# Final stage of a streaming encoder step: row scaling in two operations, its sums and low halves on POOL, and another order of loads and of the last block

## The chip, the cores and the metric

The kernel runs on one core of one Trainium2 chip. The core has five engines with a queue of their own each: PE (TensorE, matrix products), DVE (VectorE), ACT (ScalarE), POOL (GpSimd) and SP (SyncE, which here issues nearly all DMAs). Each engine works off its instructions in the order in which the program holds them, and waits for other engines on semaphores. Data lies in SBUF (128 partitions), products collect in PSUM banks of 512 fp32 columns. The metric is the device time of one execution in microseconds; less is better. One execution was also recorded by the hardware profiler, and all rows below come from that record.

## The reference

One step of a trunk layer over 2048 prompt rows and 32 sample rows of width 1024. Attention and a gated delta rule read the same normalised input; each of the two gives a branch output. What matters here is the end of the layer:

```
h   = layer_norm(x, ln0_g, ln0_b)                 # the residual stream
mix = sigmoid(gate_a) * ya + sigmoid(gate_b) * yb # two branches, each a product with its own weights
y   = layer_norm(ALPHA * h + mix @ w_out, ln_g, ln_b)
```

`ya` and `yb` are the branch operands (width 512 each) times `w_branch_a` and `w_branch_b` (512 x 1024); `w_out` is 1024 x 1024. The prompt and the sample rows pass through the same formulas with caches and states of their own.

## The kernel before, in words

Most of the span computes the input projection, the attention and the delta rule. The change lies in the last 270 us, from 1710 us on, which the program calls by these parts:

**Branch units** (`early`, `branch`). The branch operand g is loaded from memory (`glo`), cast to a high half `ghi` on ACT, and the rest `glo` is formed by a subtraction on POOL or VectorE (`split_g`). Each g buffer serves a unit: for every one of eight column tiles of 128, up to two times 256 columns, 12 products per 256 columns (whi and wlo with ghi, whi with glo). The result is multiplied on VectorE by the gate (`sg`, later `sl`), which was loaded from `sig`, and written back there. The units of the second branch still run between the first blocks of the stage below. Their PSUM bank carries the tag `b`.

**Final stage** (`merge`). The 2048 rows go in eight blocks of 256. For each of eight tiles k of 128 activation columns, `load` brings both gated branches (`sf`, 2 x 256 columns), and `fold` adds them (the sum), casts the sum to the high half `mh` on ACT and subtracts to get the low half `ml`. Sum and low half were made on VectorE for even tiles and on POOL (low half only) for odd ones. TensorE then makes, for two row tiles t and two column halves c, three products of 512 columns per k: mh with the high and the low part of `w_out`, ml with the high part. That is 96 products of 512 columns per block. The weights are `wohi`, `wolo` for k = 0 to 3 and `woh`, `wol` for k = 4 to 7. The last block also holds the 32 sample rows, with their high and low halves in one operand `ms`, 32 products.

**Banks.** PSUM tiles have the tags `a` (three banks), `c` (one), `pj` (two) and `b` (two). While branch units remain, blocks use a, a and a, c; afterwards blocks alternate between pj, b and a, c. A block's two row tiles run side by side through k, but in the last block the tiles follow each other: sample rows first, in bank b, then the first 128 rows in pj, then the others in a.

**Rows** (`x_ahead`, `x_load`, `finish`). An `xt` buffer, five in all, holds 128 rows of x. `x_load` loads them, subtracts the mean and multiplies by the reciprocal deviation (`mv`, known from the start of the kernel) on VectorE, and then scales by ln0's vectors `l0g` and `l0b`, which are already multiplied by ALPHA, in eight operations of 256 columns each: on VectorE for the first two tiles and on POOL for all others. `finish` adds the products out of PSUM to it (the eviction, which frees the bank), takes the statistics (`fst`), makes the deviation (`m`, a square root by power on POOL), scales by the final `lng` and `lnb` in two VectorE operations of 1024 columns, and stores the rows. Then the xt buffer is free for the next load.

**Weights and vectors** (`last_weights`). The second half of `w_out`, k = 4 to 7, is staged in three of the xt buffers (named `wr` then) and in the buffer of `lnb`, cast on ACT and split on POOL or VectorE. After the eight loads come l0g and l0b, and after those the first x tiles; lng and lnb come last.

**What sets the order.** The instruction stream is written at build time by a planner in Python (`Flow`). Each of the functions above is a stream that gives up control after each step; the planner always continues the stream with the smallest clock, puts its instruction at the end of the engine's queue, and moves the clocks on by a table of costs. Gates (`x_slots`, `m_slots`, `bank`) and marks hold streams back. So one change of a step can move many others in all queues. At run time nothing is reordered. All compute instructions are issued from one line, L267, and all DMAs from L290, so rows of the profile are told apart by the names of their tiles.

Of the kernel before, what the change touches and what calls it, by code (L numbers as in the profile page):

```python
# [16 lines left out]
ALU = mybir.AluOpType  # L17
# [4 lines left out]
P = 128  # L22
D = 1024
# [252 lines left out]
def trunk(ctx: ExitStack, tc: tile.TileContext, x_p, x_s, cache_k, cache_v, st_conv, st_gdn,  # L276
# [4 lines left out]
    flow = Flow()  # L281
# [1828 lines left out]
    def last_weights():  # L2110
# [20 lines left out]
        def scale(r, t, last):  # L2131
            yield t
            S.activation(out=r, in_=r, func=AF.Copy, scale=ALPHA)
            if last:
                rows_ready.done()

        stage = x_t + [rowv["lnb"][:]]
        for i in range(2 * KO, 2 * KD):
            yield from load(i // 2, i % 2, stage[i // 2 - KO][:, i % 2 * 512:(i % 2 + 1) * 512])
        for name, src in (("l0g", ln0_g), ("l0b", ln0_b)):  # L2140
            yield from row(name, src)
        flow.start(x_ahead())
        for k in range(KO, KD - 1):
# [82 lines left out]
    def early():  # L2226
        while True:
# [12 lines left out]
            for f in range(KD):  # L2240
# [5 lines left out]
                while fp_open.at is None and flow.busy["PE"] > flow.cur.clock + 0.2:  # L2246
                    yield flow.busy["PE"]
                yield bank["b"]
                ps = pt("b")
                for i, ((_, g, _), m) in enumerate(zip(what, sizes)):  # L2250
                    yield from branch(br, f, m, ps[:, i * FB:], g)

                def evac(f=f, sg=sg, slots=slots, ps=ps, t=t, c0=c0, n=n, what=what, br=br):
                    yield t + SLACK
                    V.scalar_tensor_tensor(out=sg[:, 0:n], in0=sg[:, 0:n], scalar=1.0, in1=ps[:, 0:n],
                                           op0=ALU.add, op1=ALU.mult)
                    bank["b"].give()
                    yield
                    at = dma(sig_dram[br][f][:, c0:c0 + n], sg[:, 0:n])
                    for b, _, _ in what:  # L2260
                        early_done[br, b, f].done()
                    yield at
                    slots.give()
# [21 lines left out]
    def merge():  # L2285
# [20 lines left out]
        def fold(B, f, sg, t):  # L2306
            n, x = B.n, sg[:, 0]
            yield t + SLACK / 2
            V.tensor_tensor(out=x[:, 0:n], in0=x[:, 0:n], in1=sg[:, 1, 0:n], op=ALU.add)
            yield  # L2310
            yield m_slots[f]
            eng = G if f % 2 else V
            S.copy(out=mh[f][:], in_=x[:, 0:FB])
# [56 lines left out]
        B = blocks[-1]  # L2370
        for t, name in ((2, "ba"[turn_]), (0, ("pj", "a")[turn_]), (1, ("a", "pj")[turn_])):
            yield from rows(B, (t,))
            for c in range(2):
                yield bank[name]
# [10 lines left out]
    def x_ahead():  # L2385
        n = SEQ // P
        for gt in [*range(n - 2), n, n - 2, n - 1]:
            yield x_slots
# [4 lines left out]
    def x_load(w, gt, rows):  # L2393
# [5 lines left out]
        yield rows_ready  # L2399
        V.tensor_scalar(out=xt[:rows], in0=xt[:rows], scalar1=mv[:rows, gt, 0:1],  # L2400
                        scalar2=mv[:rows, gt, 1:2], op0=ALU.subtract, op1=ALU.mult)
        yield
        eng = V if gt < 2 else G

        for name, op in (("l0g", ALU.mult), ("l0b", ALU.add)):
            for q in range(4):
                cs = slice(q * 256, (q + 1) * 256)
                eng.tensor_tensor(out=xt[:rows, cs], in0=xt[:rows, cs], in1=rowv[name][:rows, cs], op=op)
            yield
        w.ready.done()  # L2410

    def finish(w, gt, rows, c, ps, end, name):
# [11 lines left out]
        if c == 0:  # L2424
# [9 lines left out]
        yield norm_ready  # L2434
        V.scalar_tensor_tensor(out=xt[:rows], in0=xt[:rows], scalar=m2[:rows, 0:1], in1=rowv["lng"][:rows],
                               op0=ALU.subtract, op1=ALU.mult)
        yield
        V.scalar_tensor_tensor(out=xt[:rows], in0=xt[:rows], scalar=m2[:rows, 1:2], in1=rowv["lnb"][:rows],
                               op0=ALU.mult, op1=ALU.add)
        yield  # L2440
        yield dma(y_s if rows < P else y_p[gt * P:(gt + 1) * P, :], xt[:rows])
        x_slots.give()
# [99 lines left out]
```

## Time and profile before

| | us |
|---|---|
| runs shown, lowest, median, highest | 1983.57, 1983.99, 1987.36 |
| profiled execution, its time | 1980.36 |
| its span, first to last instruction | 1978.6 |
| mean granted TensorE clock | 0.988 |
| busy: PE, DVE, ACT, POOL | 1894.8, 1421.8, 993.2, 814.7 |

The profile's first section gives busy time by engine; the second the same in 40 slices of 49.5 us; the third the DMA queues; the fourth the chain of work that ended last, followed back from the last instruction; the fifth groups of instructions with mean duration, the idle time of their engine ahead of them and what ended it (the releaser). A row of the trace gives start, duration, engine, line, operation and tiles (out <- in), partitions x elements and type, and in brackets the idle time before it. A line such as `1838.56:1860.65 22.09, ...` is a stretch of the span: its length, then for each engine the busy time and the number of instructions, then the granted clock, the DMA share and GB/s.

### The profile page before, as it was taken

Reading aid. Unit: us, or ns where it says so; the run is one execution under the profiler, and the core shown is the slowest. Engines: PE = TensorE matmul, PEld = TensorE weight load, DVE = VectorE, ACT = ScalarE, POOL = GpSimd, SP = SyncE. Lnnn points to the kernel's source line nnn. Section 1 sums busy time; section 2 is a strip of 40 time slices with the busy share of each in tenths; the row PEclk is TensorE's granted clock in tenths of the full one; section 3 lists DMA queues with packets and bytes.
Section 4 is the critical chain, followed back from the end, with each engine's and each line's share of the span. In section 5 each row is a group of like instructions: output and inputs, shape, how many; then the busy total and the mean of one; then the engine's idle time right before and its main releaser. Section 6 shows DMA issues by size and latency. Waiting matters only on the chain.

```text
span 1978.6 us, 41065 instructions
## 1 busy us (share of the span) xinstructions
PE 1894.8 (96%) x14513; PEld 1338.2 (68%) x14513; DVE 1421.8 (72%) x4458; ACT 993.2 (50%) x2022; POOL 814.7 (41%) x1139
## 2 busy tenths in 40 slices
PE   8999999999999999999999999999999999989996
PEld 5455666676455556666776777678877668878874
DVE  7779989873378768579989986356466665585886
ACT  6665545444586777664544533445355774310110
POOL 7344334433344444343333432423122331363695
PEclk9999999999999999999999999999999999999998
DMA  4224242333378786223142243578878798975542
GB/s 139 68 83 125 65 108 70 84 92 108 115 159 197 188 179 156 71 79 89 52 118 68 68 112 83 139 212 192 227 173 199 168 215 177 310 272 191 167 152 83
DMA packets 382806, 274.62 MB, mean 139 GB/s; under 512 B 248322, under 2 KB 319342, under 8 KB 382600
## 3 DMA queue, kind: packets, MB, share of 16 engines
q1 hardware_dynamic: 382600, 272.00, 51.3%
q8 instruction: 114, 1.87, 0.4%
q14 instruction: 92, 0.75, 0.1%
HBM read 157.15 MB, written 71.76 MB: 116 GB/s over the span
## 4 chain that ended last, share of the span: by engine, by line
PE 64%; DVE 20%; issue 5%; ACT 4%; DMA 4%; POOL 3%; SPq 1%; POOLq 0%; DVEq 0%; ACTq 0%
PE pj L267 34%; PE b L267 15%; PE a L267 7%; PE c L267 4%; PE x L267 3%; DVE acc L267 3%; DVE sys_t L267 2%; DVE sys_u L267 2%; PE o L267 2%; DVE kd_bd L267 1%; POOL wlo L267 1%; SPq L290 1%; DVE xt L267 1%; DVE q_bd L267 1%; DMA sf<-sig 1%
## 5 line engine op out<-in xcount | busy, mean ns | idle before, releaser
L267 PE MATMUL pj<-hi,whi 128*128 128x512 f16 (+2 forms) x1992 | 642.3, 338 | 11.2 <-DVE zb L267 3.2
L267 PE MATMUL pj<-hi,wlo 128*128 128x512 f16 (+2 forms) x1952 | 633.8, 338 | 0.6 <-POOL wlo L267 0.5
L267 PEld LDWEIGHTS <-whi 128*128 128x128 f16 x3984 | 407.8, 104 | 227.3 <-issue 8.6
L267 POOL TENSOR_TENSOR wlo<-wraw,whi 128x256 f16<-128x256 f32 (+1 forms) x392 | 280.6, 738 | 460.9 <-ACT whi L267 380.5
L267 PE MATMUL pj<-lo,whi 128*128 128x512 f16 (+2 forms) x1992 | 452.5, 338 | 0.0
L267 PEld LDWEIGHTS <-wlo 128*128 128x128 f16 x1952 | 204.3, 105 | 115.2 <-issue 11.9
L267 ACT ACTIVATE sb<-sb,mx,unit 128x640 f32<-128x640 f32 (+4 forms) x128 | 108.6, 849 | 101.4 <-DVE mx L267 96.3
L267 POOL TENSOR_TENSOR pu<-sb,pu 128x640 f16<-128x640 f32 (+2 forms) x64 | 82.3, 1285 | 178.3 <-ACT pu L267 145.4
L267 ACT ACTIVATE wraw<-wraw,w_scale 128x1024 f32<-128x1024 f32 (+1 forms) x98 | 111.4, 1137 | 78.3 <-DVE w_scale L267 75.8
L267 PE MATMUL b<-ghi,whi 128*128 128x256 f32 (+1 forms) x512 | 138.7, 303 | 3.6 <-DVE cr L267 1.1
L267 ACT CAST whi<-wraw 128x512 f16<-128x512 f32 (+2 forms) x212 | 128.2, 611 | 27.5 <-PE pj L267 24.6
L267 PE MATMUL b<-ghi,wlo 128*128 128x256 f32 (+1 forms) x512 | 129.5, 284 | 0.0
L267 DVE TENSOR_TENSOR sys_u<-sys_u,sys_t 128x60 f32<-128x60 f32 (+24 forms) x527 | 124.6, 242 | 5.7
L267 DVE SCALAR_TENSOR_TENSOR acc<-raw,cwT,acc 128x512 f32<-128x512 f32 x144 | 112.7, 782 | 7.9 <-ACT acc L267 6.5
L267 ACT CAST mh<-sf 128x256 fp32r<-128x256 f32 x64 | 25.7, 406 | 178.8 <-PE c L267 74.8
L267 DVE TENSOR_TENSOR sys_t<-sys_u,sys_p 128x60 f32<-128x60 f32 (+21 forms) x459 | 109.8, 242 | 5.5
L267 PEld LDWEIGHTS b<-ghi,whi 128*128 128x128 f32 x512 | 97.3, 190 | 9.7 <-ACT ghi L267 1.5
L267 ACT COPY v_t<-o 128x64 f32<-128x64 f32 x132 | 27.7, 210 | 143.2 <-PE o L267 106.7
L267 PEld LDWEIGHTS b<-ghi,wlo 128*128 128x128 f32 x512 | 97.5, 190 | 1.5
L267 DVE CUSTOM_DVE_ANT_0 sb<-a,bias 128x320 f32<-128x320 f32 (+5 forms) x136 | 66.2, 497 | 45.0 <-PE a L267 42.4
L267 POOL TENSOR_TENSOR w_scale<-w_scale,mhalf 128x1 f32<-128x1 f32 x49 | 32.2, 657 | 157.3 <-DVE w_scale L267 113.8
L267 ACT ACTIVATE sig<-pj,w_half 128x512 f32<-128x512 f32 (+2 forms) x84 | 49.3, 587 | 77.0 <-PE pj L267 71.6
(377 smaller groups left out, 4097.7 us busy)
## 6 DMA issues: line engine op xcount, KB each, us to landing
wraw<-in_w_in SPq DMA_DIRECT2D x192, 256.0 KB
sf<-sig SPq DMA_DIRECT2D x112, 128.0 KB
sig<-sig SPq DMA_DIRECT2D x44, 256.0 KB
sg<-sig SPq DMA_DIRECT2D x37, 256.0 KB
sig<-sg SPq DMA_DIRECT2D x37, 256.0 KB
sys_p<-sol_p SPq DMA_DIRECT2D x68, 128.0 KB
x<-in_x_p SPq DMA_DIRECT2D x16, 512.0 KB
xt<-in_x_p SPq DMA_DIRECT2D x16, 512.0 KB
```

The source lines that it names most:

```text
L267: r = f(*a, **k)
L290: eng.dma_start(dst, src)
```

## The change

Five things are changed, all in the last 270 us:

- `x_load`: the scaling of a tile is two VectorE operations of 1024 columns, (x - mean) * l0g and then times reciprocal deviation plus l0b, for all tiles. POOL has no part in it.
- `fold`: from the second block on, all low halves are made on POOL, and the sums of odd tiles too.
- `last_weights`: l0g and l0b are loaded first and the x tiles are started ahead of the weights of k = 4 to 7. `x_ahead` also puts the sample rows behind one more prompt tile.
- `merge` and `early`: the last block runs the first 128 rows, then the sample rows, then the other 128 rows; branch units use the pj banks once the input projection is done with them (`jobs_done`).
- `finish`: the very last tile's scaling and store go in two halves of 512 columns.

```diff
@@ -2134,12 +2134,12 @@
             if last:
                 rows_ready.done()
 
+        for name, src in (("l0g", ln0_g), ("l0b", ln0_b)):
+            yield from row(name, src)
+        flow.start(x_ahead())
         stage = x_t + [rowv["lnb"][:]]
         for i in range(2 * KO, 2 * KD):
             yield from load(i // 2, i % 2, stage[i // 2 - KO][:, i % 2 * 512:(i % 2 + 1) * 512])
-        for name, src in (("l0g", ln0_g), ("l0b", ln0_b)):
-            yield from row(name, src)
-        flow.start(x_ahead())
         for k in range(KO, KD - 1):
             yield w_ready["o", k, 1]
             x_slots.give()
@@ -2245,16 +2245,17 @@
                         yield m
                 while fp_open.at is None and flow.busy["PE"] > flow.cur.clock + 0.2:
                     yield flow.busy["PE"]
-                yield bank["b"]
-                ps = pt("b")
+                name = "b" if jobs_done.at is None else "pj"
+                yield bank[name]
+                ps = pt(name)
                 for i, ((_, g, _), m) in enumerate(zip(what, sizes)):
                     yield from branch(br, f, m, ps[:, i * FB:], g)
 
-                def evac(f=f, sg=sg, slots=slots, ps=ps, t=t, c0=c0, n=n, what=what, br=br):
+                def evac(name=name, f=f, sg=sg, slots=slots, ps=ps, t=t, c0=c0, n=n, what=what, br=br):
                     yield t + SLACK
                     V.scalar_tensor_tensor(out=sg[:, 0:n], in0=sg[:, 0:n], scalar=1.0, in1=ps[:, 0:n],
                                            op0=ALU.add, op1=ALU.mult)
-                    bank["b"].give()
+                    bank[name].give()
                     yield
                     at = dma(sig_dram[br][f][:, c0:c0 + n], sg[:, 0:n])
                     for b, _, _ in what:
@@ -2306,10 +2307,10 @@
         def fold(B, f, sg, t):
             n, x = B.n, sg[:, 0]
             yield t + SLACK / 2
-            V.tensor_tensor(out=x[:, 0:n], in0=x[:, 0:n], in1=sg[:, 1, 0:n], op=ALU.add)
+            (G if B.b and f % 2 else V).tensor_tensor(out=x[:, 0:n], in0=x[:, 0:n], in1=sg[:, 1, 0:n], op=ALU.add)
             yield
             yield m_slots[f]
-            eng = G if f % 2 else V
+            eng = G if B.b or f % 2 else V
             S.copy(out=mh[f][:], in_=x[:, 0:FB])
             B.ready[0][f].done()
             yield
@@ -2368,9 +2369,9 @@
             for (t, c), ps in pss.items():
                 end(B, t, c, ps, names[t][c])
         B = blocks[-1]
-        for t, name in ((2, "ba"[turn_]), (0, ("pj", "a")[turn_]), (1, ("a", "pj")[turn_])):
+        for t, names in ((0, ("pj pj", "a a")[turn_]), (2, ("b b", "a c")[turn_]), (1, ("a a", "pj pj")[turn_])):
             yield from rows(B, (t,))
-            for c in range(2):
+            for c, name in enumerate(names.split()):
                 yield bank[name]
                 ps = pt(name)
                 for k in range(KD):
@@ -2384,7 +2385,7 @@
 
     def x_ahead():
         n = SEQ // P
-        for gt in [*range(n - 2), n, n - 2, n - 1]:
+        for gt in [*range(n - 1), n, n - 1]:
             yield x_slots
             w = Rows()
             flow.start(x_load(w, gt, P if gt < SEQ // P else DEC))
@@ -2397,16 +2398,12 @@
 
         yield dma(xt[:rows], x_s if rows < P else x_p[gt * P:(gt + 1) * P, :]) + 3.0
         yield rows_ready
-        V.tensor_scalar(out=xt[:rows], in0=xt[:rows], scalar1=mv[:rows, gt, 0:1],
-                        scalar2=mv[:rows, gt, 1:2], op0=ALU.subtract, op1=ALU.mult)
+        V.scalar_tensor_tensor(out=xt[:rows], in0=xt[:rows], scalar=mv[:rows, gt, 0:1], in1=rowv["l0g"][:rows],
+                               op0=ALU.subtract, op1=ALU.mult)
         yield
-        eng = V if gt < 2 else G
-
-        for name, op in (("l0g", ALU.mult), ("l0b", ALU.add)):
-            for q in range(4):
-                cs = slice(q * 256, (q + 1) * 256)
-                eng.tensor_tensor(out=xt[:rows, cs], in0=xt[:rows, cs], in1=rowv[name][:rows, cs], op=op)
-            yield
+        V.scalar_tensor_tensor(out=xt[:rows], in0=xt[:rows], scalar=mv[:rows, gt, 1:2], in1=rowv["l0b"][:rows],
+                               op0=ALU.mult, op1=ALU.add)
+        yield
         w.ready.done()
 
     def finish(w, gt, rows, c, ps, end, name):
@@ -2432,13 +2429,16 @@
         rsqrt(m2[:rows, 1:2], m2[:rows, 1:2])
         yield
         yield norm_ready
-        V.scalar_tensor_tensor(out=xt[:rows], in0=xt[:rows], scalar=m2[:rows, 0:1], in1=rowv["lng"][:rows],
-                               op0=ALU.subtract, op1=ALU.mult)
-        yield
-        V.scalar_tensor_tensor(out=xt[:rows], in0=xt[:rows], scalar=m2[:rows, 1:2], in1=rowv["lnb"][:rows],
-                               op0=ALU.mult, op1=ALU.add)
-        yield
-        yield dma(y_s if rows < P else y_p[gt * P:(gt + 1) * P, :], xt[:rows])
+        dst = y_s if rows < P else y_p[gt * P:(gt + 1) * P, :]
+        for q in ((slice(0, 512), slice(512, D)) if end else (slice(0, D),)):
+            V.scalar_tensor_tensor(out=xt[:rows, q], in0=xt[:rows, q], scalar=m2[:rows, 0:1], in1=rowv["lng"][:rows, q],
+                                   op0=ALU.subtract, op1=ALU.mult)
+            yield
+            V.scalar_tensor_tensor(out=xt[:rows, q], in0=xt[:rows, q], scalar=m2[:rows, 1:2], in1=rowv["lnb"][:rows, q],
+                                   op0=ALU.mult, op1=ALU.add)
+            yield
+            at = dma(dst[:, q], xt[:rows, q])
+        yield at
         x_slots.give()
         if end:
             all_done.done()
```

The planner then writes the queues in another order. Three places follow. The first is TensorE at the end of block 0, whose last operands are mh_21961 and ml_21969, where ghi and whi are operands of a branch unit. Before:

```order
L267 MATMUL c<-woh_21913,mh_21961 128x512
L267 MATMUL c<-wol_21917,mh_21961 128x512
L267 MATMUL a<-woh_21913,ml_21969 128x512 x3
L267 MATMUL c<-woh_21913,ml_21969 128x512
L267 MATMUL b<-ghi,whi_19664 128x256
L267 MATMUL b<-ghi,wlo_19665 128x256
```

48 branch products in bank b stand here before block 1's first product, a<-wohi_21760,mh_21954. After:

```order
L267 MATMUL c<-woh_21913,mh_21961 128x512
L267 MATMUL c<-wol_21917,mh_21961 128x512
L267 MATMUL a<-woh_21913,ml_21969 128x512 x3
L267 MATMUL c<-woh_21913,ml_21969 128x512
L267 MATMUL a<-wohi_21760,mh_21954 128x512
L267 MATMUL a<-wolo_21761,mh_21954 128x512
```

Block 1 follows block 0 at once, in the same banks; after 16 of its products, 22 behind the branch unit before, the next branch unit comes, in pj.

The second is SP's queue of DMA issues where the weights of k = 4 to 7 (wr) are loaded; sig, sg, sl and sf are stores and loads of gated branches. Removed rows have a minus, added ones a plus:

```order
-L290 DMA wr<-in_w_out 128x512 x4
+L290 DMA l0g<-in_ln_g 128x1024
+L290 DMA l0b<-in_ln_b 128x1024
 L290 DMA sig_72<-sg 128x512
-L290 DMA wr<-in_w_out 128x512 x2
+L290 DMA wr<-in_w_out 128x512
+L290 DMA xt<-in_x_p 128x1024 x2
+L290 DMA wr<-in_w_out 128x512
 L290 DMA sig_73<-sl 128x512
 L290 DMA sf<-sig_73 128x256
```

The ln0 vectors and two x tiles now stand among the first weight loads, and the other weight loads come later in the queue.

The third is POOL in one block of the steady part. Before, with m the deviations, xt the scaling of x, ml the low halves:

```order
L267 TENSOR_TENSOR m_23552<-m_23552,mhalf 128x1
L267 TENSOR_TENSOR m_23566<-m_23566,mhalf 128x1
L267 TENSOR_TENSOR xt<-xt,l0g 128x256 x4
L267 TENSOR_TENSOR ml_21965<-sf,mh_21957 128x256
L267 TENSOR_TENSOR xt<-xt,l0b 128x256 x4
L267 TENSOR_TENSOR xt<-xt,l0g 128x256 x4
L267 TENSOR_TENSOR ml_21967<-sf,mh_21959 128x256
L267 TENSOR_TENSOR xt<-xt,l0b 128x256 x4
L267 TENSOR_TENSOR ml_21969<-sf,mh_21961 128x256
L267 TENSOR_TENSOR ml_21963<-sf,mh_21955 128x256
```

After, with sf<-sf the sums:

```order
L267 TENSOR_TENSOR ml_21965<-sf,mh_21957 128x256
L267 TENSOR_TENSOR ml_21966<-sf,mh_21958 128x256
L267 TENSOR_TENSOR sf<-sf 128x256
L267 TENSOR_TENSOR ml_21967<-sf,mh_21959 128x256
L267 TENSOR_TENSOR ml_21968<-sf,mh_21960 128x256
L267 TENSOR_TENSOR sf<-sf 128x256
L267 TENSOR_TENSOR ml_21969<-sf,mh_21961 128x256
L267 TENSOR_TENSOR ml_21962<-sf,mh_21954 128x256
L267 TENSOR_TENSOR sf<-sf 128x256
L267 TENSOR_TENSOR ml_21963<-sf,mh_21955 128x256
L267 TENSOR_TENSOR m_23673<-m_23673,mhalf 128x1
L267 TENSOR_TENSOR m_23685<-m_23685,mhalf 128x1
```

The sixteen scalings are gone; four more low halves and four sums stand in their place.

## The prediction, made before the changed kernel was run

> **What bounds the kernel now.** I read the slices first (TensorE at nine tenths almost to the end), then the chain that ended last (TensorE carries it), then busy time by stretches of the last 270 us, then TensorE's own rows there. Stretches, with columns PE, PEld, DVE, ACT and POOL busy, granted clock, DMA share, GB/s:
>
> ```profile
> 1710.00:1750.00 40.00, 38.95 (x246) 34.64 (x245) 25.71 (x44) 14.11 (x32) 14.75 (x15) 1.00 0.97 325
> 1762.00:1772.30 10.30, 4.41 (x10) 3.48 (x11) 10.23 (x19) 1.63 (x5) 10.30 (x14) 0.67 0.65 208
> 1838.56:1860.65 22.09, 22.09 (x98) 18.03 (x97) 18.81 (x29) 3.26 (x8) 19.40 (x21) 1.00 0.33 102
> 1926.75:1947.94 21.19, 11.62 (x33) 5.83 (x32) 15.59 (x25) 1.69 (x7) 12.87 (x19) 0.68 0.37 123
> 1947.94:1970.24 22.30, 22.30 (x97) 17.83 (x95) 15.22 (x21) 0.00 (x0) 16.45 (x17) 1.00 0.20 77
> ```
>
> The third row is one block of 256 rows: 22.09 us, TensorE without a gap. The second and fourth are two places where it starves while VectorE and POOL work. Its own rows there, idle time and releaser in brackets:
>
> ```profile
> 1729.43 0.39 PE L267 MATMUL b<-ghi,whi 128*128 128x256 f32 x1 [0.71 <-ACT ghi L267]
> ...
> 1761.53 0.40 PE L267 MATMUL a<-wolo,mh 128*128 128x512 f32 x1
> 1767.89 0.80 PE L267 MATMUL a<-wohi,mh 128*128 128x512 f32 x1 [5.97 <-DVE xt L267]
> ...
> 1783.61 0.39 PE L267 MATMUL b<-ghi,whi 128*128 128x256 f32 x1 [0.88 <-DVE sl L267]
> ...
> 1927.90 0.40 PE L267 MATMUL b<-wolo,ms 128*64 128x512 f32 x1
> 1934.24 0.69 PE L267 MATMUL b<-wohi,ms 128*64 128x512 f32 x1 [5.95 <-POOL ms L267]
> ...
> 1940.69 0.69 PE L267 MATMUL b<-woh,ms 128*64 128x512 f32 x1 [3.63 <-DVE ms L267]
> ```
>
> And the chain, in order of time:
>
> ```profile
> 1785.53 1.43 PE b L267 x12
> ...
> 1924.23 2.86 POOL xt L267 x5
> ...
> 1931.04 2.93 POOL xt L267 x4
> ...
> 1948.11 11.07 PE pj L267 x48
> 1959.17 11.08 PE a L267 x48
> ```
>
> A product of 512 columns costs 11.07 / 48 = 0.231 us, so TensorE's losses can be counted. Place 1, start of block 1: idle 5.97, then ten products in 4.41 instead of 2.31 at the clock of 0.67: 8.1. Place 2, at 1783: 0.88, and 0.3 because the twelve after it are slow: 1.2. Place 3, the sample rows: six of 32 products done at 1928.13, the other 26 end at 1947.94, 19.8 us for 6.0 us of work: 13.8. Together 23.1 us, and nothing else between 1762 and the end is lost. In place 3 the chain runs through POOL's scaling of x; the low halves of the sample rows (ms) stand behind it.
>
> **Why places 1 and 3 exist.** Prices on VectorE, the last two reading PSUM or one operand:
>
> ```profile
> 1825.67 0.75 DVE L267 TENSOR_TENSOR sf<-sf 128x256 f32<-128x256 f32 x2
> ...
> 1820.06 2.48 DVE L267 SCALAR_TENSOR_TENSOR xt<-xt,m,lng 128x1024 f32<-128x1024 f32 x2
> ...
> 1790.88 0.81 DVE L267 TENSOR_SCALAR xt<-xt,mv 128x1024 f32<-128x1024 f32 x1
> ...
> 1813.24 1.88 DVE L267 SCALAR_TENSOR_TENSOR xt<-a,xt 128x512 f32<-128x512 f32 x3
> ...
> 1815.64 2.46 DVE L267 BATCH_NORM_STATS2 fst<-xt 128x6 f32<-128x512 f32 x4
> ```
>
> and on POOL, with two VectorE rows from the time of the fourth, and the shortest, median and longest lng in ns:
>
> ```profile
> 1798.14 3.01 POOL L267 TENSOR_TENSOR xt<-xt,l0g 128x256 f32<-128x256 f32 x4
> ...
> 1813.45 0.73 POOL L267 TENSOR_TENSOR ml<-sf,mh 128x256 fp32r<-128x256 f32 x1 [8.63 <-PE c L267]
> ...
> 1819.20 1.35 POOL L267 TENSOR_TENSOR m<-m,mhalf 128x1 f32<-128x1 f32 x2 [5.02 <-DVE m L267]
> ...
> 1915.02 9.04 POOL L267 TENSOR_TENSOR xt<-xt,l0g 128x256 f32<-128x256 f32 x4 [2.08 <-DVE xt L267]
> ...
> 1916.48 1.27 DVE L267 SCALAR_TENSOR_TENSOR xt<-xt,m,lng 128x1024 f32<-128x1024 f32 x1
> ...
> 1919.58 2.46 DVE L267 SCALAR_TENSOR_TENSOR xt<-xt,m,lnb 128x1024 f32<-128x1024 f32 x2
> ...
> L267 DVE SCALAR_TENSOR_TENSOR xt<-xt,m,lng x17: 1265/1273/1829, 1773.9 to 1972.0; 128x1024 f32<-128x1024 f32 x16, 32x1024 f32<-32x1024 f32 x1
> ```
>
> POOL's four take 3.01 us alone and 9.04 beside VectorE's operations on two SBUF operands, which keep their 1.24; beside evictions out of PSUM its 0.73 stays. So I count operations of the first sort as taking turns with POOL, evictions and statistics (1.88 + 0.63 + 2.46, and some 0.7 of small ones: 5.7 us a block) as free.
>
> **The sum by parts.** *x scaling, sums and low halves.* Per block before, VectorE in turns: 8 sums x 0.375 + 4 lows x 0.375 + 2 x 0.81 + 4 x 1.24 = 11.1 us; POOL: 16 scalings x 0.75 + 4 lows x 0.75 + two square roots 1.35 = 16.4. Together 27.5 against 22.09: every block falls 5.4 behind, and five blocks back from 1926.75 make 27. The stall of 13.8 is what tiles scaled ahead and buffers did not cover; they covered about 13. After: VectorE 4 sums 1.5 + 8 x 1.24 = 11.4; the new scaling has the form of the lng and lnb operations, and I take their 1.24 (ends 1.27 and 1.83, the extremes of the row below). POOL: 8 lows + 4 sums, 12 x 0.75 + 1.35 = 10.4. Together 21.8 against 22.09. The two just fit, VectorE alone has 17.1 of 22.09, and place 3 should go: take 0, keep 0 and 9.5 as ends (24.0 a block, a tenth of the turns wasted, five blocks, no cover). Lows of all eight tiles now queue on POOL, and ACT's casts and the sf loads wait for POOL's; each has one block period between free and needed, so I cost that at nothing; without that cover it is the 9.5.
>
> *Last block's order.* The sample rows now follow 48 products of the first 128 rows, so all eight ms have 11.07 us more. mh of tile 7 is needed 14 products (3.2 us) into the block, and a cast and a low take some 1.2 us (a cast of twice the width took 0.62). This costs nothing by itself; it is the cover for a lag of some 10 us at ms, but not at mh.
>
> *ln0 vectors and two x tiles ahead of w_out.* SP and ACT there, TensorE's first products with the weights of tiles 4 and 5, and the operand g of the branch units, twice:
>
> ```profile
> 1711.77 1.34 SPq L290 DMA_DIRECT2D wr<-in_w_out  x2
> 1717.09 0.62 ACT L267 CAST woh<-wr 128x512 fp32r<-128x512 f32 x1 [0.87 <-DMA wr<-in_w_out]
> ...
> 1724.92 0.39 PE L267 MATMUL a<-woh,mh 128*128 128x512 f32 x1
> ...
> 1727.65 0.39 PE L267 MATMUL a<-woh,mh 128*128 128x512 f32 x1
> ...
> 1722.69 1.17 SPq L290 DMA_DIRECT2D glo<-g  x2
> 1728.98 1.33 ACT L267 CAST ghi<-glo 128x256 fp32r<-128x256 f32 x4 [3.49 <-DMA glo<-g]
> ...
> 1766.90 0.37 SPq L290 DMA_DIRECT2D glo<-g  x1
> 1770.36 1.32 ACT L267 CAST ghi<-glo 128x256 fp32r<-128x256 f32 x4
> 1774.33 2.29 POOL L267 TENSOR_TENSOR glo<-glo,ghi 128x256 fp32r<-128x256 f32 x2
> ```
>
> x is ready before block 0 ends, so the wait of place 1 for scaling goes. But the moved loads are 2 MB on DMA engines that are 97% busy, and the weights of tiles 4 to 7 come later. A weight half is cast 5.3 us after its issue (1711.77 to 1717.09), and split 1.3 later. Tile 4 lands by about 1723, needed at 1724.9: free. Tile 5's halves now stand on SP right before the two glo loads of 1722.69 (so near 1723) and seven issues behind them, at 0.4 to 0.7 each near 1728: usable near 1729.7 and 1734.6, while TensorE comes for them near 1727.7 and, 36 branch products later (1.43 per twelve), 1733.7. Part of that it waits for ghi anyway. Cost 1.5, ends 0 and 5.3 (one whole landing).
>
> *Branch units in the pj banks.* Same two banks, same operations, but the order changes: before, 48 branch products stood between blocks 0 and 1, now block 1 follows at once. Its four banks are freed by four evictions of 0.63 each, against 0.46 for each pair of products: 0.8 us of waits. Then the next unit comes after only 22 products of 512 columns, 5.9 us after the g buffers come free with those waits, but after 0.5 of issue a load took 3.1 to 5.1 us to land (4.1), then 1.32 of casts and 2.29 of splits: ready at about 8.2, partly covered by its own first eight products, so 1.0 of wait, and 0.4 of slow clock. Place 1 becomes 2.2 (ends 0.8 and 8.1). Place 2 stays in kind: an eviction stands on VectorE behind the second g's splits and an lng: 1.5 (ends 0 and 3).
>
> A wait of 0.88 left the clock at 1.00 and one of 5.97 brought it to 0.67; mine lie between. The Trainium skill, page "TensorE: Matmul & The Clock Gate", section "HAM oscillation — how this bites in real kernels", puts the limit at idle gaps of about 3.4 us; by it my waits keep the clock, and if they joined to one gap above that they would cost the 2.1 of place 1 again: 15.8 in place of 17.9.
>
> *Tail.* The last rows' scale and bias go in halves, with two stores. VectorE does one half-width operation more before the last store (0.6, half of 1.24), and that store is half as long: 0, ends -0.7 and 0.7.
>
> Sum: 23.1 - 1.5 - 2.2 - 1.5 = 17.9 us gained. The profiled execution took 1980.36 us with a span of 1978.6 and should become 1962.5; the median of the runs shown lies 3.6 above it, so the time is 1983.99 - 17.9 = 1966.1.
>
> **Rivals.** *The end still waits.* 21.8 of 22.09 leaves no room; at 24.0 a block the lag of 9.5 reaches the last block's mh: 1975.6. For it: two in-order queues seldom mesh; against: before, 13 us of lag were covered, and the new order of the last block covers ms. *The weights are late.* The second and third thing moved ahead of them delays tile 5 or 6 by a whole landing more, 5.3: 1971.4. For it the DMA share of 0.97; against it, tiles 6 and 7 are needed only after five more branch units of 24 products. *POOL is starved (slower).* VectorE's eight scalings come in one chain of about 10 us per block, and the 9.04 row says what POOL gets beside such a chain: 2.26 an operation. Twelve of those and two square roots at the 1.46 seen below:
>
> ```profile
> 1972.27 1.46 POOL L267 TENSOR_TENSOR m<-m,mhalf 128x1 f32<-128x1 f32 x1 [7.88 <-DVE m L267]
> ```
>
> make 30.0 a block, 7.9 behind, 40 over five, less 13 of cover: 27 at the end instead of 13.8, and the 4.1 gained in places 1 and 2 don't pay for it: 1983.99 + 13 - 4 = 1993. It decides from 2.1 us per POOL operation. Against it: VectorE leaves POOL 10.7 us of each block free. The Trainium skill, page "SBUF — State Buffer", section "Who interferes with whom", has this as a rule: who issues first holds the shared port for a whole instruction and the other engine blocks entirely, also for a VectorE operation with two SBUF inputs. The rows at 1915 and 1916 agree. *No change:* both of the first two together, and a cold clock again: gain under 4.
>
> **How the numbers follow.** Forecast 0.62; end still waits 0.15; weights late 0.10; no change 0.06; starved 0.07. Within 0.2% (4 us, about what a measurement tells from no change) counts as same: faster 0.87, same 0.06, slower 0.07. If all of 23.1 went and the tail gave 0.7, 1960.2; the range runs from 1961 to the "end still waits" case, 1976.
>
> **What would show it.** In the profile after: no wait of TensorE for xt at the start of block 1 above 2 us, waits below 3 us each between 1725 and 1790; from block 2 to the last product no gap; ms off the list of releasers; POOL operations at a mean near 0.9 us; VectorE at 17 to 20 us a block. Wrong would be: blocks longer than 22.1 us, POOL above 2 us an operation, TensorE waiting for woh or wol.

## The result and the profile after

The changed kernel ran at a median of 1966.28 us (1963.54 to 1968.59, 4 runs), the kernel before at 1985.67 us (1983.57 to 1988.43): a ratio of 0.9904, interval 0.9885 to 0.9924. The forecast was 1966.1.

The two medians lie 19.4 us apart and the two profiled executions only 13.4 (spans of 1965.2 and 1978.6 us), and the reason matters for all that follows. Up to the last group of attention products all engines hold the same program in both kernels. TensorE's row of that group in the timeline, before and then after:

```profile
1687.82 0.60 PE L267 MATMUL c<-vt,pt 128*128 128x64 f16 x15
```

```profile
1693.39 0.60 PE L267 MATMUL c<-vt,pt 128*128 128x64 f16 x15
```

The same work arrived 5.57 us later in the second execution. From that row to the end of the span it is 1978.6 - 1687.82 = 290.8 us before and 1965.2 - 1693.39 = 271.8 after: 19.0 us gained in the part that was changed. I use this distance, called the stage, for every kernel below. The changed kernel, profiled a second time, gave 272.1.

TensorE's waits after the change, from the first product of block 0:

```profile
1714.69 0.51 PE L267 MATMUL a<-wohi,mh 128*128 128x512 f32 x1 [0.47 <-ACT mh L267]
...
1733.77 0.50 PE L267 MATMUL a<-woh,mh 128*128 128x512 f32 x1 [0.64 <-ACT woh L267]
1735.74 0.50 PE L267 MATMUL a<-wol,mh 128*128 128x512 f32 x1 [1.47 <-DVE wol L267]
...
1777.62 0.39 PE L267 MATMUL pj<-ghi,whi 128*128 128x256 f32 x1 [0.58 <-DVE sl L267]
...
1781.03 0.38 PE L267 MATMUL pj<-ghi,whi 128*128 128x256 f32 x1 [0.33 <-DVE sl L267]
```

The waits of 5.97 for xt, 5.95 and 3.63 for ms are gone; new is a place at the weights of k = 5. Stretches after (columns as before: PE, PEld, DVE, ACT, POOL, clock, DMA, GB/s), the weights, block 6 and the last block:

```profile
1732.97:1741.85 8.88, 6.77 (x39) 6.25 (x39) 6.51 (x8) 4.51 (x12) 6.40 (x8) 0.81 1.05 368
...
1905.50:1927.60 22.10, 22.10 (x98) 18.04 (x97) 18.03 (x25) 4.21 (x16) 17.91 (x20) 1.00 0.53 176
1927.60:1957.10 29.50, 29.49 (x128) 21.96 (x127) 27.16 (x40) 0.00 (x0) 5.05 (x6) 1.00 0.16 65
```

and the end of the chain of waits, which is the last block alone:

```profile
1927.60 14.75 PE a L267 x64
1942.34 3.68 PE c L267 x16
1946.02 11.08 PE pj L267 x48
```

In the last block TensorE runs without a gap: 128 products in 29.5 us, 0.231 each. What POOL and VectorE do meanwhile shows in the groups from 1800 to 1920 (count, busy us, mean ns, idle time and releasers), three rows of POOL before, then POOL and VectorE after:

```profile
L267 POOL TENSOR_TENSOR xt<-xt,l0g 128x256 f32<-128x256 f32 x28 | 32.7, 1194 | 7.5 <-DVE xt L267 7.5
L267 POOL TENSOR_TENSOR xt<-xt,l0b 128x256 f32<-128x256 f32 x28 | 26.0, 958 | 0.0
L267 POOL TENSOR_TENSOR ml<-sf,mh 128x256 fp32r<-128x256 f32 x19 | 15.9, 842 | 27.7 <-PE c L267 24.5 <-PE b L267 3.1
```

```profile
L267 POOL TENSOR_TENSOR ml<-sf,mh 128x256 fp32r<-128x256 f32 x39 | 40.7, 1044 | 44.7 <-PE c L267 28.1 <-PE b L267 16.1 <-DMA sf<-sig 0.4
L267 POOL TENSOR_TENSOR sf<-sf 128x256 f32<-128x256 f32 (+1 forms) x19 | 22.5, 1182 | 3.2 <-DMA sf<-sig 3.1
...
L267 DVE SCALAR_TENSOR_TENSOR xt<-xt,mv,l0g 128x1024 f32<-128x1024 f32 x8 | 12.4, 1548 | 0.0
L267 DVE SCALAR_TENSOR_TENSOR xt<-xt,mv,l0b 128x1024 f32<-128x1024 f32 x8 | 12.2, 1524 | 0.0
```

The idle time is the telling column. POOL waits for TensorE (the slots of ml) for as long as it is ahead of it: 27.7 us before, 44 after. What differs most is when these waits end. The last one before, and the last one after, which stands at the end of block 6:

```profile
1888.47 0.74 POOL L267 TENSOR_TENSOR ml<-sf,mh 128x256 fp32r<-128x256 f32 x1 [0.28 <-PE b L267]
```

```profile
1927.74 0.74 POOL L267 TENSOR_TENSOR ml<-sf,mh 128x256 fp32r<-128x256 f32 x1 [1.40 <-PE b L267]
```

So before, POOL lost its lead near 1888, some 38 us ahead of place 3; after, it keeps it through the steady blocks.

### The profile page after: what moved, and what is told of

It reads as the page before. It is cut to its first block, busy times and chain, and to the rows that moved or that the text cites. A ratio compares the mean times of both kernels' runs of the same rounds, so it can differ in the third digit from the quotient of the medians.

```text
span 1965.2 us, 40968 instructions
## 1 busy us (share of the span) xinstructions
PE 1894.8 (96%) x14513; PEld 1339.0 (68%) x14513; DVE 1409.0 (72%) x4401; ACT 993.6 (51%) x2022; POOL 771.2 (39%) x1079
## 5 line engine op out<-in xcount | busy, mean ns | idle before, releaser
L267 ACT COPY v_t<-o 128x64 f32<-128x64 f32 x132 | 27.7, 210 | 142.1 <-PE o L267 105.5
L267 PE MATMUL b<-ghi,whi 128*128 128x256 f32 (+1 forms) x320 | 89.3, 311 | 1.2 <-DVE cr L267 1.1
L267 POOL TENSOR_TENSOR ml<-sf,mh 128x256 fp32r<-128x256 f32 x60 | 59.5, 993 | 77.3 <-PE c L267 51.5
L267 ACT CAST pu<-sb 128x640 f16<-128x640 f32 (+4 forms) x128 | 82.2, 650 | 0.7
L267 PEld LDWEIGHTS <-pt 128*128 128x128 f16 x1680 | 65.8, 98 | 23.3 <-issue 6.0
```

Source lines behind the costliest of these rows:

```text
L267: r = f(*a, **k)
```

## The experiments

Theories named in the expectations: mine (POOL and VectorE take turns on operations of two SBUF operands, and a block falls behind when the turns exceed 22.09 us), and rivals A to I, each told where it stands. A ratio is against runs of the kernel before on the same chip. Each stage comes from one profile, and the two profiles of the changed kernel differ by 0.3, so a difference of that size says nothing.

| kernel | median us | ratio to before, interval | span | last attention products | stage |
|---|---|---|---|---|---|
| before | 1985.67 | 1 | 1978.6 | 1687.82 | 290.8 |
| changed | 1966.28 | 0.9904 (0.9885 to 0.9924) | 1965.2 | 1693.39 | 271.8 |
| e1 old scaling and sums | 1979.32 | 0.9969 (0.9958 to 0.9981) | 1978.8 | 1694.70 | 284.1 |
| e2 old last block | 1967.78 | 0.992 (0.9899 to 0.994) | 1968.3 | 1696.09 | 272.2 |
| e3 old loads | 1968.99 | 0.9922 (0.9905 to 0.994) | 1967.3 | 1694.06 | 273.2 |
| e4 old sums and low halves | 1965.52 | 0.9911 (0.9894 to 0.9927) | 1962.0 | 1689.91 | 272.1 |
| e5 before, new scaling only | 1966.20 | 0.99 (0.9873 to 0.9927) | 1966.9 | 1692.55 | 274.4 |
| e6 before, new last block only | 1980.55 | 0.9972 (0.9958 to 0.9985) | 1979.3 | 1694.25 | 285.0 |
| e7 four weights first | 1967.96 | 0.9907 (0.9881 to 0.9933) | 1961.5 | 1692.16 | 269.3 |
| e8 old scaling, new sums | 2003.72 | 1.0092 (1.0069 to 1.0116) | 2001.2 | 1691.44 | 309.8 |
| e9 changed, again | 1969.69 | 0.9919 (0.9905 to 0.9933) | 1967.8 | 1695.71 | 272.1 |
| e10 old bank | 1967.54 | 0.9905 (0.9891 to 0.9918) | 1966.1 | 1692.08 | 274.0 |
| e11 weights, then g, then x | 1965.37 | 0.9894 (0.988 to 0.9907) | 1962.1 | 1693.25 | 268.8 |
| e12 e11 with the old bank | 1966.36 | 0.9914 (0.9884 to 0.9943) | 1964.1 | 1696.64 | 267.5 |

**e1, the old scaling in the changed kernel.** `x_load` and `fold` as before, the rest changed:

```diff
-        V.scalar_tensor_tensor(out=xt[:rows], in0=xt[:rows], scalar=mv[:rows, gt, 0:1], in1=rowv["l0g"][:rows],
-                               op0=ALU.subtract, op1=ALU.mult)
+        V.tensor_scalar(out=xt[:rows], in0=xt[:rows], scalar1=mv[:rows, gt, 0:1],
+                        scalar2=mv[:rows, gt, 1:2], op0=ALU.subtract, op1=ALU.mult)
...
+        eng = V if gt < 2 else G
+        for name, op in (("l0g", ALU.mult), ("l0b", ALU.add)):
+            for q in range(4):
...
-            eng = G if B.b or f % 2 else V
+            eng = G if f % 2 else V
```

> Changed kernel, but rows are scaled by ln0 on POOL and sums and low halves are made as before (the load order, pj banks, last block's order and tail stay). Measured from the last attention product (same instruction in all kernels) to the end of the span: before 290.8, after 271.8. My theory (POOL and VectorE take turns; 27.5 us of turns against 22.09 a block): every block falls behind by about 5 again; the new order of the last block hides up to 11 of the lag of ms, so 4 to 14 us come back: 276 to 286, with TensorE waiting in the last two blocks for a tile made behind POOL's scaling. Rival A (the new order of the last block alone cured the wait at the sample rows): 271 to 273. Rival B (the loads did it all, x early): 271 to 273 too, with no wait at the end.

Measured 284.1. TensorE, VectorE, ACT and POOL at the last block:

```profile
1940.45 0.50 PE L267 MATMUL a<-woh,mh 128*128 128x512 f32 x1 [2.56 <-ACT mh L267]
...
1942.01 0.67 PE L267 MATMUL a<-woh,mh 128*128 128x512 f32 x1 [0.82 <-ACT mh L267]
```

```profile
1930.77 3.44 DVE L267 SCALAR_TENSOR_TENSOR xt<-xt,m,lnb 128x1024 f32<-128x1024 f32 x2
1934.14 0.99 DVE L267 TENSOR_TENSOR sf<-sf 128x288 f32<-128x288 f32 x1
...
1935.24 0.41 ACT L267 CAST mh<-sf 128x256 fp32r<-128x256 f32 x1 [8.70 <-DVE sf L267]
...
1929.73 5.99 POOL L267 TENSOR_TENSOR xt<-xt,l0b 128x256 f32<-128x256 f32 x4
```

12.3 of the 19.0 us come back, as my theory had it. The late tiles are now those of mh: POOL's four operations take 5.99 in place of some 3, beside VectorE's chain, and the sum and the cast stand behind that chain. The last block starts 240.3 into the stage instead of 234.2 and takes 35.8 to TensorE's last product instead of 29.5, so half of the loss is there and half in front, where TensorE waits longer for weights and branch units (1.02, 0.88, 1.21 and 1.93). The wait for xt at block 1 is only 0.47. Rivals A and B fall.

**e2, the old last block in the changed kernel.** `for t, name in ((2, "ba"[turn_]), (0, ...), (1, ...))` and the x tiles in the old order.

> Changed kernel with the old order of the last block (sample rows first, in bank b) and of its x tiles. My theory: the steady blocks no longer fall behind, so ms are ready when block 6 ends; 0 to 1.5 us lost, 272 to 273.5 from the last attention product to the end. Rival A (the order of the last block is what cured the wait): TensorE waits for ms again, 6 to 14 us: 278 to 286.

Measured 272.2, and TensorE has no wait for ms. With blocks that keep up the order of the last one is worth 0.4 at most, hardly more than two profiles of one kernel differ. Rival A falls again.

**e3, the old load order in the changed kernel.** The two lines that load l0g and l0b, and `flow.start(x_ahead())`, stand behind the loop over the weights again.

> Changed kernel with l0g, l0b and the first x tiles behind all weights of w_out, as before. My theory: TensorE's wait before block 1 for scaled rows comes back (6 to 8 us with the clock), and the wait for the weights of k = 5 (4.2 us with the slow products behind it, in the trace after) goes: 2 to 4 us slower, 274 to 276. Rival C (two operations in place of nine scale rows early enough whatever the load order): the weights' 4.2 gone and nothing in exchange, 267 to 269.

Measured 273.2, 1.1 to 1.4 slower than the two profiles of the changed kernel, between the two expectations:

```profile
1736.88 0.39 PE L267 MATMUL pj<-ghi,whi 128*128 128x256 f32 x1 [1.91 <-ACT ghi L267]
...
1766.05 0.50 PE L267 MATMUL a<-wohi,mh 128*128 128x512 f32 x1 [1.84 <-DVE xt L267]
```

The wait for xt at block 1 is 1.84 in place of 5.97 although the loads are late: two operations instead of nine are enough for most of the cure of place 1. The weights' wait is gone, but TensorE then waits for ghi in the same place, which rival C left out.

**e4, the old sums and low halves in the changed kernel.** The two lines of `fold` as before; the scaling stays new.

> Changed kernel with sums on VectorE and low halves split evenly, as before; rows still scaled on VectorE in two operations. My theory of turns: VectorE 8 x 0.375 + 4 x 0.375 + 8 x 1.24 = 14.4, POOL 4 x 0.75 + 1.35 = 4.4, together 18.8 of 22.09, less than the 21.8 of the changed kernel: no loss, 271 to 273. Rival D (VectorE, with its 5.7 of evictions and statistics at 20.1 of 22.09, is too full and falls behind): a wait of 3 to 10 us in the last blocks, 275 to 282.

Measured 272.1, as the turns said. This part of the change brought nothing: VectorE had the room, and rival D falls.

**e5, only the new scaling in the kernel before.** The `x_load` of the change, nothing else.

> Kernel before with only the new scaling of x (two VectorE operations, nothing of it on POOL); sums, low halves, loads, banks, last block and tail as before. From the last attention product to the end: before 290.8, changed kernel 271.8. My theory: turns per block 14.4 + 4.4 = 18.8 of 22.09, so the blocks keep up, the wait at the sample rows (13.8) goes, and the wait before block 1 shrinks because two operations are shorter than nine: 272 to 277, most of the whole gain. Rival A (the last block's order cures the end): the wait at ms stays, 284 to 288.

Measured 274.4, 16.4 of the 19.0 us from one part of five, with the sample rows still first in the last block:

```profile
1763.41 0.50 PE L267 MATMUL a<-wohi,mh 128*128 128x512 f32 x1 [1.47 <-DVE xt L267]
...
1781.95 0.58 PE L267 MATMUL b<-glo,whi 128*128 128x256 f32 x1 [2.04 <-DVE glo L267]
...
1932.07 0.45 PE L267 MATMUL a<-woh,ms 128*64 128x512 f32 x1 [0.54 <-POOL ms L267]
```

The waits for ms, 9.58 together, are 0.54.

**e6, only the new last block in the kernel before.** The loop over `names` and the order of `x_ahead` of the change, nothing else.

> Kernel before with only the new order of the last block and of its x tiles. My theory: the lag stays, ms is covered by the 48 products ahead, but mh of the last tiles is not; about 6 us are lost in the last block as in the kernel with the old scaling, instead of 13.8: 282 to 285. Rival A (the order cures the end): 276 to 278.

Measured 285.0, 5.8 gained, at the upper edge of my range, with the wait moved from ms to mh:

```profile
1774.21 0.79 PE L267 MATMUL a<-wohi,mh 128*128 128x512 f32 x1 [5.97 <-DVE xt L267]
...
1942.37 0.80 PE L267 MATMUL pj<-woh,mh 128*128 128x512 f32 x1 [5.94 <-ACT mh L267]
```

e2, e5 and e6 together: the order hides a lag in part, the scaling removes it, and with the lag gone there is little left to hide.

**e8, POOL overloaded.** The changed kernel with the old `x_load` and the new `fold`, so POOL has scaling, all low halves and half of the sums.

> Changed kernel with x scaled on POOL as before, while the low halves of all tiles and half of the sums stay on POOL too. Theory of turns: VectorE 4 x 0.375 + 2 x 0.81 + 4 x 1.24 = 8.1, POOL 28 x 0.75 + 1.35 = 22.4, together 30.5 against 22.09, 3.0 a block more than with the old split (27.5): 12 to 18 us more than the 284.1 of that kernel, 296 to 302. Rival G (each engine counts by itself; they disturb each other little): POOL's 22.4 just reaches the block's 22.09, 0 to 3 us more: 284 to 287.

Measured 309.8; the run is slower than the kernel before. TensorE, then two stretches:

```profile
1944.17 0.80 PE L267 MATMUL a<-woh,mh 128*128 128x512 f32 x1 [7.41 <-ACT mh L267]
1951.36 0.80 PE L267 MATMUL a<-woh,mh 128*128 128x512 f32 x1 [5.97 <-ACT mh L267]
1963.85 0.79 PE L267 MATMUL a<-woh,mh 128*128 128x512 f32 x1 [11.26 <-ACT mh L267]
```

```profile
1859.00:1903.00 44.00, 44.00 (x193) 35.91 (x192) 30.79 (x42) 5.24 (x14) 43.48 (x50) 1.00 0.52 168
...
1944.00:1964.00 20.00, 2.60 (x5) 1.16 (x5) 14.58 (x15) 1.29 (x6) 20.00 (x25) 0.50 0.23 82
```

Rival G (every engine counts by itself) falls by 23 us. My number was too small by 8 as well. POOL is busy 43.48 of the 44.00 us of two blocks and makes 50 operations in them, where 60 are due (28 and two square roots a block): 10 at 0.87, 4.3 us a block behind while TensorE still lives on what was made ahead. From 1937 on, where the first of the three waits begins, it has nothing left and POOL sets the pace. That POOL takes 0.87 here and 0.75 alone is, as I read it, the price of the turns. The sum of turns gets the sign, not the size: by it POOL would be 8.4 behind a block (30.5 - 22.09), and it is 4.3.

**e7, four weight halves first.** In the changed kernel:

```diff
-        for name, src in (("l0g", ln0_g), ("l0b", ln0_b)):
-            yield from row(name, src)
-        flow.start(x_ahead())
         stage = x_t + [rowv["lnb"][:]]
         for i in range(2 * KO, 2 * KD):
+            if i == 2 * KO + 4:
+                for name, src in (("l0g", ln0_g), ("l0b", ln0_b)):
+                    yield from row(name, src)
+                flow.start(x_ahead())
             yield from load(i // 2, i % 2, stage[i // 2 - KO][:, i % 2 * 512:(i % 2 + 1) * 512])
```

> Changed kernel with the four weight halves of k = 4 and 5 loaded first, then l0g, l0b, the x tiles, and the other weights. My theory: the wait for the weights of k = 5 goes (4.2 us with the slow products behind it), but a wait of about 2 us for the branch operand ghi stays in that place, as in the kernel with all weights first, and rows are still scaled in time: 1 to 3 us faster, 269 to 271. Rival E (the place is bound by the branch operand alone): 271 to 272. Rival F (x comes too late again before block 1): 272 to 274.

Measured 269.3, in the range of my theory, though the wait of about 2 us is not the one that I named: nothing waits for weights or ghi, and one wait for the split of g (glo) is left there. Rivals E and F fall. TensorE, and what stood on VectorE ahead of it:

```profile
1740.27 0.92 PE L267 MATMUL pj<-glo,whi 128*128 128x256 f32 x3 [2.23 <-DVE glo L267]
```

```profile
1736.47 1.75 DVE L267 SCALAR_TENSOR_TENSOR xt<-xt,mv,l0b 128x1024 f32<-128x1024 f32 x1
1738.14 1.74 DVE L267 SCALAR_TENSOR_TENSOR xt<-xt,mv,l0g 128x1024 f32<-128x1024 f32 x1
1739.81 0.74 DVE L267 TENSOR_TENSOR glo<-glo,ghi 128x256 fp32r<-128x256 f32 x2
```

Two scalings of rows that nobody needs before 1762 stand in VectorE's queue ahead of a split for which TensorE waits.

**e9, the changed kernel again,** for comparison with e10 and e11 on one chip.

> The changed kernel itself, once more, beside the next two on the same chip: 271.8 plus or minus 0.5 from the last attention product to the end, whatever the part before that product takes; the time itself between 1963 and 1970.

Measured 272.1, with a median of 1969.69, both in their ranges.

**e10, the old bank in the changed kernel.** `bank["b"]` for all branch units.

> Changed kernel with the branch units in bank b as before, so that 48 of their products stand between the blocks 0 and 1 again. My theory: the four evictions of block 0 are hidden behind these again, no wait for rows either since they are scaled early, and the short waits of 0.58 and 0.33 on the gated product (sl) change places: 270.5 to 272.5. Rival H (the pj order is what keeps TensorE fed between blocks 0 and 3): 1.5 to 4 us slower, 273.3 to 276.

Measured 274.0, in the range of rival H. But TensorE's largest wait in it is 3.35 for woh of k = 5, where the changed kernel has 2.18 (e9) or 0.64 and then 1.47 for wol, and the order of the loads is the same. e12 takes that wait out.

**e11, weights, then g, then x.** As e7, with `flow.start(x_ahead())` one half later (`i == 2 * KO + 5`). The planner then writes the x loads behind the loads of g, and the scalings behind the splits.

> Changed kernel with the four weight halves of k = 4 and 5 first, then l0g and l0b, and the first x tiles only behind the fifth half, which puts them behind the branch operand g in SP's queue and behind its splits on VectorE. My theory: the 2.23 us that TensorE waited for the split of g behind a scaling of x (kernel with weights first) shrink to under 1, with the slow products behind it: 1.5 to 3 us faster than that kernel's 269.3, 266.5 to 268. Rival F (x comes too late before block 1 again): a wait of 1 to 3 us there for xt, 268.5 to 272.

Measured 268.8, 0.5 less than e7 where I had 1.3 to 2.8; the wait on glo shrinks from 2.23 to 0.37 and xt costs 0.29:

```profile
1739.67 0.50 PE L267 MATMUL pj<-glo,whi 128*128 128x256 f32 x2 [0.37 <-POOL glo L267]
...
1763.64 0.50 PE L267 MATMUL a<-wohi,mh 128*128 128x512 f32 x1 [0.29 <-DVE xt L267]
```

The number lies in the range of rival F, but the wait of 1 to 3 us for xt that F needs is not there. So the mechanism held and the size did not; other small waits took up the rest. Beside the changed kernel on the same chip its median is 1965.37 against 1969.69, and its stage 268.8 against 272.1: 3 to 4 us better. The intervals of the two ratios, 0.988 to 0.9907 and 0.9905 to 0.9933, only just overlap.

**e12, e11 with the old bank.**

> The kernel with the four weight halves first and x behind g (268.8), but with the branch units in bank b as before the change. The old bank alone gave 274.0 against 271.8 and 272.1, but over 1 us of that was a longer wait for the weights of k = 5, which don't wait here. My theory: what is left is one wait for rows before block 1 and one on the gated product, 1 us together: 269.3 to 270.3. Rival I (the bank made no difference, the 2 us were the landing of the weights): 268.3 to 269.2. Rival H (the new bank is worth its whole 2 us): 270.5 to 271.5.

Measured 267.5, below all three expectations and nearest to rival I. So, as far as one profile each can show it, the old bank costs nothing where the weights are there in time; rival H falls, and the 2 us of e10 were not the bank's own price. By the stage this is the best version, 4.3 below the changed kernel; by the times, with an interval of 0.9884 to 0.9943, it can't be told from e11.

## Why the prediction was right, point by point

**The steady blocks and place 3: right in sign, not in size.** 13.8 us were to go and went. The decisive step was the count of turns, 27.5 against 22.09 before and 21.8 after. e1 and e5 put the loss on the scaling, and e8 shows that POOL's load at the price it has alone (22.4 against 22.09) doesn't give it. In every kernel the sign is the one of the count: 27.5 and 30.5 fall behind, 18.8 and 21.8 do not. The size isn't shown. The lag did not grow by 5.4 in each of five blocks: POOL still waited for TensorE until 1888, and the 13 us of cover that the prediction took off were found from the same stall that they were to explain. That the two engines slow each other is in the rows: POOL's operations took 1.19 and 0.96 before, and VectorE's sums (sf) a mean of 652 ns from 1800 to 1920 before and 439 in e5, where POOL scales nothing. But no run tells the turns from the plain order of POOL's queue, in which a low half stands behind eight scalings; the new scaling removes both. Two details were off. The changed split was said to just fit; e4, with 18.8 turns, is no faster, so 21.8 was not at an edge. And POOL's operations were to take about 0.9 us; they took 1.04 and 1.18, and VectorE's scalings 1.52 to 1.55 in place of 1.24: both engines pay, which the forecast put on POOL alone. VectorE had the room (18.03 of 22.10 in block 6). The starved case, from 2.1 us per operation, was far off.

**Last block's order: right.** Costed at nothing and as cover for ms but not for mh. e6 and e1 show that: the wait moves to mh, 5.94 and 2.56 + 0.82.

**Late weights: near in size, by errors that cancel.** Predicted 1.5 (ends 0 and 5.3). The prediction named TensorE waiting for woh or wol as a sign that it would be wrong, and there it was. The place on SP was right: the first half of k = 5 was put near 1723 on the clock of the trace before, which is 1728.6 in the trace after. Rows of SP, ACT and VectorE after:

```profile
1729.04 0.42 SPq L290 DMA_DIRECT2D wr<-in_w_out  x1
...
1733.10 0.62 ACT L267 CAST woh<-wr 128x512 fp32r<-128x512 f32 x1 [1.53 <-DMA wr<-in_w_out]
...
1731.05 1.75 DVE L267 SCALAR_TENSOR_TENSOR xt<-xt,mv,l0b 128x1024 f32<-128x1024 f32 x1
...
1734.48 1.21 DVE L267 TENSOR_TENSOR wol<-wr,woh 128x512 fp32r<-128x512 f32 x1
```

The half was cast 4.1 after its issue, sooner than the 5.3 I took. But its split stands on VectorE behind a scaling of x, a sum and a low half (both 0.95 there), starts 1.4 after the cast does, and takes 1.21. So the half was usable 6.65 after its issue, where I had 6.6: a quicker landing made up for a queue that I had not followed, since I followed the moved scaling through SP's queue and not through VectorE's. That is luck.

What I put at nothing is the clock. It fell behind the two waits, to 0.81 over the stretch: two products and three units of twelve took from 1732.97 to 1741.85, 8.9 us for 2 x 0.233 + 3 x 1.41 = 4.7. That is 4.2 lost, by the starts of the products 2.5 in the two waits and the rest in slow products. The kernel before lost something in this place too, between these products and with 24 branch products among them:

```profile
1728.33 0.39 PE L267 MATMUL a<-wol,mh 128*128 128x512 f32 x1
...
1734.10 0.40 PE L267 MATMUL c<-woh,mh 128*128 128x512 f32 x1
```

These 5.77 us hold 3 x 0.233 + 2 x 1.41 = 3.5 of work, so 2.2 were lost before, at a clock of 1.00, which is more than the two waits of 0.71 and 0.30 for g. The net cost is 2.0 where 1.5 was forecast. The waits for the weights replaced those for g almost one for one; the step that failed is that the prediction let its waits keep the clock.

**Place 1: over-costed.** Predicted 2.2 left of 8.1. No wait on a semaphore shows, but the four evictions do:

```profile
1768.61 0.50 PE L267 MATMUL a<-wohi,mh 128*128 128x512 f32 x1
...
1769.20 0.50 PE L267 MATMUL a<-wohi,mh 128*128 128x512 f32 x1
...
1769.80 0.50 PE L267 MATMUL a<-wohi,mh 128*128 128x512 f32 x1
...
1770.40 0.50 PE L267 MATMUL c<-wohi,mh 128*128 128x512 f32 x1
```

The pairs follow at 0.60 instead of 0.46, with 0.27 ahead of the first: 0.7, where 0.8 was costed. The wait for g, 1.0 and 0.4 for the clock, did not come; it is 0.3. So 1.0 is left. The prediction gave the credit for the cure to the early loads. They do it without the new scaling (a wait of 0.47 in e1), but the two operations do most of it without the early loads (1.84 in e3, 1.47 in e5). Either is enough, and beside the new scaling the loads are worth 1.1 to 1.4.

**Place 2:** predicted 1.5, measured 1.4: by the starts of the products 0.74 and 0.50 at the waits of 0.58 and 0.33, and some 0.2 of slower products. **Tail:** predicted 0, measured 8.36 to 8.10 from TensorE's last product to the end, 0.3 gained; kernels e5 and e6, with the old tail, have 8.3 and 8.7, the others 8.0 or 8.1.

Together 23.1 - 2.0 - 1.0 - 1.4 + 0.3 = 19.0 from the rows, which is what the stage gained, with the weights 0.5 dearer, places 1 and 2 1.3 cheaper and the tail 0.3 better than forecast. So the forecast rested on one large term that was right and on small ones that erred by about 1 us together.

That the time came within 0.2 us of 1966.1 is luck. The median of the kernel before is 1985.67 beside the changed one, 1.7 above the 1983.99 from which the forecast was taken, and the gain is 19.4 in place of 17.9.

## What to carry to other kernels

When two engines share work on the same rows, add up their time per block as if they took turns before you split the load between them, and trust the sign of the sum more than its size; here moving work to the faster engine and shortening it gave 16 of 19 us, and evening out the load gave none. A reordering that hides a lag is worth little once the lag is gone, so find the lag first. When you start some work earlier, follow it through every queue that it enters, the compute queue too: a weight split and a split of g each waited behind rows scaled some 25 us or more ahead of need.

## What was unexpected of the hardware

The clock fell after shorter waits than I assumed. In all fourteen traces the granted clock changes only at instants that lie whole multiples of 3.41 us apart, and a slow stretch has a clock of 0.50. Here are the waits of 1.91 and 1.84 in e3, cut at these instants (behind the length stands TensorE's busy time, ahead of the DMA share the granted clock):

```profile
1732.90:1736.31 3.41, 2.07 (x10) 1.37 (x8) 0.00 (x0) 0.00 (x0) 1.73 (x3) 1.00 1.02 350
1736.31:1739.73 3.42, 2.81 (x16) 2.40 (x17) 2.57 (x4) 2.86 (x9) 2.83 (x4) 1.00 1.03 375
...
1763.62:1767.03 3.41, 1.57 (x11) 1.28 (x11) 3.41 (x5) 0.00 (x0) 2.29 (x2) 1.00 0.93 305
1767.03:1770.45 3.42, 3.42 (x16) 3.23 (x16) 3.42 (x6) 0.00 (x0) 0.64 (x1) 0.50 0.78 249
```

The wait of 1.91 fell across two such windows and left the clock at 1.00; that of 1.84 lay in one, and the next window ran at 0.50. In e5 a wait of 1.47 left TensorE 1.94 us busy in its window and the clock at 1.00, and one of 2.04 left 1.42 and brought 0.50. Over all fourteen traces, from the last attention products to TensorE's last product, a window at full clock with at most 0.55 of it busy was always followed by a slow one, and one with 0.64 or more never; in between it went both ways. So where a wait falls matters as much as its length. The Trainium skill, page "TensorE: Matmul & The Clock Gate", section "HAM oscillation — how this bites in real kernels", puts the limit at idle gaps of about 3.4 us, by which none of these would have cost any clock; the measurement decides, and here waits from about 1.8 us can, though not each does.

The part ahead of the change, the same program in every kernel, ended between 1687.82 and 1696.64 us in these fourteen profiles. A spread of 8.8 us is nearly half of what was to be measured, and a landmark inside the trace takes it out.
